# The scratch of queries, keys, values and gates stored in the order in which the attention stage reads it

## The chip, the cores and the metric

The kernel runs on one NeuronCore of a Trainium2 chip. The metric is device time of one execution in microseconds (us). Every engine has its own queue: TensorE (PE, with its weight loads as PEld), VectorE (DVE), ScalarE (ACT), GpSimd (POOL) and SyncE (SP). SP computes nothing here; it issues nearly all DMA transfers, in a fixed order, and a transfer whose data or buffer isn't ready holds up everything behind it on SP.

## What is computed

One decoder layer on x of 1024 positions by 1024 channels, in float32, and a final RMSNorm. What matters for this change is the attention branch; the rest is the work around it.

```
proj = h @ w_in[l]                       # h: x normed, scaled, shifted
q, k, v, g_attn, xr, g_rnn, m_attn, m_rnn = split(proj)
q = partial_rope(q, positions)           # 16 heads of 64, the first 16 columns turned
k = partial_rope(k, positions)           # 4 key heads; 4 query heads share each
y_attn = sliding_window_attention_with_sinks(q, k, v, sinks) * silu(g_attn)
y_rnn  = rg_lru(causal_conv(xr), ...) * silu(g_rnn)
merged = sigmoid(m_attn) * (y_attn @ w_attn_proj) + sigmoid(m_rnn) * (y_rnn @ w_rnn_proj)
out = rmsnorm(x + gate * (merged @ w_out), final_g)
```

The window is 128 positions: a block of 128 queries sees the keys of its own block and of the block before.

## The kernel before

**Numbers.** A float32 matrix is used as a high part, rounded to float32r, plus a low part, the rest; a product is made of three matmuls (high by high, low by high, high by low). That is why ACT (high parts, L100 and L102) and DVE (low parts, L106 and L108) work all the time beside PE.

**Stages.** The start (0 to about 97 us) norms and transposes x and makes the keys, v and the first gate products. Then a long run of products (`Pair`, `run`, L647) makes everything that comes from `w_in`, a pair of 128-column chunks at a time, with steps for ACT, DVE and SP hung on slots (`at_slot`). The queries of the four groups g come first in it (up to about 210 us), the attention gates from 433 to 586 us. From about 560 us the attention runs, 32 units u of one group and one block of 128 queries, and between its steps the last products and then the projection of the other branch (`rp_steps`, L169) fill PE. After 750 us come the attention projection, the merge and the output projection (L1707).

**The order of the work** is written out: each engine runs its instructions in the order in which the code issues them, and a group of instructions on different engines is tied by semaphores. SP's transfers take turns on eight semaphores (DMAHW0 to DMAHW7 in the rows below), so that a transfer isn't issued before the one eight places ahead of it has landed. POOL's transfers do the same (DMASW).

**Scratch in HBM.** Results that a later stage needs are stored to HBM and loaded again:

- `k_d` [512, 1024]: the keys of all heads, rows 0 to 255 high parts and 256 to 511 low parts. Written by `rope_a` and `rope_b` (L561, L577): each call makes 128 rows by 512 positions of a high part (`rhi`, ACT, L583) and of a low part (`rlo`, DVE, L587) and stores both.
- `q_d[g]` [512, 1024]: the same for the queries of group g.
- `vs_d[g]`, `dv_d[g]` [128, 8, 128]: v and the difference between v and v of the block before, made by `v_prep` (L1119), which reads v back from `v_d`.
- `ga_d[g]` [2, 128, 1024]: the gates, stored by `tanh_sinks` (L752) through `store`.

`rhi` and `rlo` have two buffers each, so the third `rhi` can be made only when the store of the first has landed. The same ACT queue then makes high parts of weights, for which DVE and PE wait.

**Loads of the attention** (L1165 to L1183). `load_kq(m)` serves two units. The keys of one head are 64 rows in `ks`; they are needed in all 128 partitions, once beside the high and once beside the low parts of the queries, so two transfers load the same data into partitions 0 to 63 and 64 to 127, in pieces of 256 or 384 positions (1.0 or 1.5 KB). `qs` is loaded in pieces of 256 positions (1 KB), four to a partition. `load_v(m)` loads `dv` and `vs` from POOL's queue, in pieces of 512 B to 1 KB. `load_gq(m)` (L1395) loads gates in pieces of 1 KB. `scores` (L1190) multiplies them: per unit eight matmuls, whose moving operand is 256 keys in one stretch of `ks`. The rows y of the other branch (`yh`, `yl`, `load_y`, L1307) and its weights (`load_r`) are loaded on SP in between.

Of the kernel before, what the change touches and what calls it, by code (L numbers as in the profile page):

```python
# [22 lines left out]
P = 128  # L23
# [5 lines left out]
NG = 4  # L29
# [22 lines left out]
def tile_hybrid_block(ctx, tc, x, pk, rows, posr, posi, invf, c_row, w_ss, w_gate, w_main, w_v,  # L52
# [506 lines left out]

    def rope_a(src, th, dst):  # L560
# [17 lines left out]
    def rope_b(src, th, dst, r0=P):  # L578
# [6 lines left out]
        def f2():  # L585
            t["l"] = rpp.tile([P, HALF], F32R, tag="rl", name="rlo", bufs=2)
            V.tensor_tensor(out=t["l"][:], in0=src(), in1=f32(t["h"][:]), op=ALU.subtract)  # L587
            dma(dst[r0:r0 + P, SL[th]], t["h"][:])
            dma(dst[r0 + 2 * P:r0 + 3 * P, SL[th]], t["l"][:])
# [134 lines left out]
    def rope_q(g):  # L724
        return {"C11": lambda s: rope_a(s, 0, q_d[g]), "C12": (blk, lambda s: rope_a(
                    s, 1, q_d[g])),
                "C21": lambda s: rope_b(s, 0, q_d[g]), "C22": (blk, lambda s: rope_b(
                    s, 1, q_d[g])), "late": 11}
# [24 lines left out]
    def tanh_sinks(dst, silu, own=False):  # L753
        def steps(j, th):
            def sink(s):
# [361 lines left out]
    def v_prep(g):  # L1117
# [19 lines left out]
        def f3():  # L1137
            for n_, d_, dst in (("v", "vs", vs_d), ("d", "dv", dv_d)):
# [26 lines left out]
    def load_kq(m):  # L1165
        g, t0 = m // 4, (m % 4) * 256
        ks = W["kq"].tile([P, 2, 384], F32R, tag="ks", name="ks")
        kv = k_d.rearrange("(b a r j) t -> j (a r) b t", b=2, a=2, r=32, j=4)[g]
        lo = P if t0 == 0 else 0
        for rep in range(2):  # L1170
            dma(ks[rep * 64:(rep + 1) * 64, :, lo:], kv[:, :, t0 - P + lo:t0 + 256])
        qs = W["kq"].tile([P, 4, 256], F32R, tag="qs", name="qs")
        dma(qs[:], q_d[g].rearrange("(a j) t -> a j t", j=4)[:, :, t0:t0 + 256])
        U["kq", m] = ks, qs

    def load_v(m):
        g, n0 = m // 4, (m % 4) * 2
        vs = at.tile([P, 2, P], F32R, tag="vs", name="vs", bufs=2)
        dv = at.tile([P, 2, P], F32R, tag="dv", name="dv", bufs=2)
# [662 lines left out]
```

## Time and profile before

| | |
|---|---|
| median of 3 runs | 936.0 us (935.87, 936.0, 938.92) |
| the profiled execution | 940.08 us, of which 938.4 us from the first to the last instruction |
| PE busy | 916.0 us (98%) |
| PEld, DVE, ACT, POOL busy | 756.6, 678.8, 541.2, 125.9 us |
| granted TensorE clock, mean | 0.993 |
| moved by DMA | 164.73 MB in 80691 packets, mean 176 GB/s |

Times in the trace count from the first instruction. In a table of windows a row gives a stretch of time: for each engine its busy time and in brackets the number of instructions, then the granted TensorE clock (PEclk, 1.00 is full), the mean busy share of the 16 DMA engines (it can read a little over 1) and the GB/s that they moved. In a list of waits a row names the engine and instruction that sat idle, what it waited for, the idle time in total, how often, and the longest. A timeline row gives start, duration, engine, line and operation, and in square brackets the idle time before it and what ended it. SPq is SP's issuing of transfers. A matmul's end is modelled; with nothing to wait for, the matmuls of 128x512 start 0.23 us apart.

### The profile page before, as it was taken

How to read it: one execution, taken by the hardware profiler on the slowest of the kernel's cores; microseconds unless marked ns; L12 is line 12 of the kernel's file. 1: busy time of each engine (PE TensorE's matmuls, PEld its weight loads, DVE VectorE, ACT ScalarE, POOL GpSimd, SP SyncE). 2: the span in 40 equal slices, each digit the busy share in tenths (PEclk: the TensorE clock that was granted, in tenths of full speed). 3: DMA queues.
4: the chain of work that ended last, by engine and by line, in shares of the span. 5: the costliest groups of instructions: out<-in, count | busy, mean ns of one | idle time of the engine just before them, and what ended most of it. 6: DMA issues, size and time to landing. Idle time of an engine off the chain costs nothing.

```text
span 938.4 us, 12480 instructions
## 1 busy us (share of the span) xinstructions
PE 916.0 (98%) x4285; PEld 756.6 (81%) x4285; DVE 678.8 (72%) x999; ACT 541.2 (58%) x1050; POOL 125.9 (13%) x227
## 2 busy tenths in 40 slices
PE   6999989999999999999999999999999999999997
PEld 5689878788888888888888888887888888888886
DVE  5998587786668955985697697898999737656522
ACT  6866544555556855866595875887887622212311
POOL 4720050000000000000000001444454300000000
PEclk9899999999999999999999999999999999999999
DMA  9815577472332443352435158998656186436321
GB/s 350 337 56 202 180 258 236 143 254 108 113 113 90 145 135 102 120 203 67 136 107 188 68 200 249 324 352 226 216 175 188 57 321 216 162 131 218 133 76 68
DMA packets 80691, 164.73 MB, mean 176 GB/s; under 512 B 12418, under 2 KB 28818, under 8 KB 80628
## 3 DMA queue, kind: packets, MB, share of 16 engines
q1 hardware_dynamic: 77876, 156.59, 49.4%
q0 software_dynamic: 2608, 7.09, 2.3%
q8 instruction: 34, 0.56, 0.2%
q14 instruction: 29, 0.24, 0.1%
q10 hardware_dynamic: 144, 0.26, 0.1%
HBM read 114.52 MB, written 49.78 MB: 175 GB/s over the span
## 4 chain that ended last, share of the span: by engine, by line
PE 79%; DMA 9%; DVE 6%; ACT 3%; issue 2%; SPq 0%; POOL 0%; DVEq 0%; ACTq 0%
PE bk L647 42%; PE rp L169 8%; PE pgate L956 5%; PE rp L1707 5%; PE pmain L1707 4%; PE s_ps L1200 3%; PE pmain L453 2%; PE pv L1273 2%; PE bk L453 2%; DMA tt<-tr_d 1%; DMA wo<-w_out 1%; DMA yl<-yl_d 1%; PE pt L1239 1%; DMA r<-w_rp 1%; DMA ks<-k_d 1%
## 5 line engine op out<-in xcount | busy, mean ns | idle before, releaser
L647 PE MATMUL bk<-nl,wh 128*128 128x512 f32 x368 | 144.5, 393 | 0.0
L647 PE MATMUL bk<-nh,wh 128*128 128x512 f32 x368 | 144.5, 393 | 0.0
L647 PE MATMUL bk<-nh,wl 128*128 128x512 f32 x368 | 143.6, 390 | 0.0
L106 DVE TENSOR_TENSOR wl<-r,wh 128x512 fp32r<-128x512 f32 x109 | 78.4, 726 | 13.1 <-ACT wh L100 13.1
L100 ACT CAST wh<-r 128x512 fp32r<-128x512 f32 x105 | 64.5, 618 | 34.7 <-DMA r<-w_ap 10.6
L647 PEld LDWEIGHTS bk<-nh,wl 128*128 128x128 f32 x368 | 69.1, 188 | 15.6
L647 PEld LDWEIGHTS bk<-nl,wh 128*128 128x128 f32 x368 | 69.1, 188 | 15.3
L647 PEld LDWEIGHTS bk<-nh,wh 128*128 128x128 f32 x368 | 69.2, 188 | 15.2 <-ACT wh L102 0.9
L647 PE MATMUL bk<-hl,wh 128*128 128x512 f32 x184 | 72.2, 393 | 0.0
L647 PE MATMUL bk<-hh,wh 128*128 128x512 f32 x184 | 72.2, 392 | 0.0
L647 PE MATMUL bk<-hh,wl 128*128 128x512 f32 x184 | 71.7, 390 | 0.0
L106 DVE TENSOR_TENSOR wl<-ws,wh 128x512 fp32r<-128x512 f32 x76 | 51.4, 682 | 4.8 <-ACT wh L100 4.8
L1225 ACT ACTIVATE p<-p,small 128x129 f32<-128x129 f32 x128 | 50.1, 401 | 0.0
L100 ACT CAST wh<-ws 128x512 fp32r<-128x512 f32 x76 | 45.7, 615 | 3.0 <-DVE ws L669 1.5
L821 POOL MEMSET xr<- 128x3 f32 x8 | 0.8, 100 | 313.2 <-PE pgate L956 232.8
L647 PEld LDWEIGHTS bk<-hl,wh 128*128 128x128 f32 x184 | 34.6, 188 | 7.7
L647 PEld LDWEIGHTS bk<-hh,wl 128*128 128x128 f32 x184 | 34.6, 188 | 7.7
L647 PEld LDWEIGHTS bk<-hh,wh 128*128 128x128 f32 x184 | 34.6, 188 | 7.2
L647 PE MATMUL bk<-hha,wl 128*128 128x512 f32 x92 | 36.9, 401 | 3.4 <-DVE wl L106 2.7
L1200 PE MATMUL s_ps<-ks,qs 128*128 128x256 f32 (+1 forms) x256 | 37.6, 289 | 0.3 <-DVE p L1215 0.3
L647 PE MATMUL bk<-hla,wh 128*128 128x512 f32 x92 | 36.8, 400 | 0.0
L760 ACT ACTIVATE c<-bk 128x512 f32<-128x512 f32 x29 | 17.3, 596 | 33.7 <-PE bk L647 33.7
(351 smaller groups left out, 2276.4 us busy)
## 6 DMA issues: line engine op xcount, KB each, us to landing
r<-w_main SPq DMA_DIRECT2D x100, 256.0 KB, 4.2
wada<-w_ss SPq DMA_DIRECT2D x16, 512.0 KB, 8.6
qs<-q_d SPq DMA_DIRECT2D x16, 512.0 KB, 5.6
ks<-k_d SPq DMA_DIRECT2D x24, 192.0 KB, 4.1
xt<-x SPq DMA_DIRECT2D x8, 512.0 KB, 8.2
sma_d<-c SPq DMA_DIRECT2D x16, 256.0 KB, 2.9
wg<-w_gate SPq DMA_DIRECT2D x8, 512.0 KB, 4.8
q_d<-rhi SPq DMA_DIRECT2D x16, 256.0 KB, 4.8
```

The costliest lines, as they stand in the source:

```text
L100: A.copy(dst[0][:], src)
L106: V.tensor_tensor(out=dst[1][:], in0=src, in1=f32(dst[0][:]), op=ALU.subtract)
L169: mm = T.matmul(ps[hf], ww, xx[kc][hf], start=(kc == 0 and ww is w_h and xx is xh), stop=(kc == KC - 1 and xx is xl))
L453: T.matmul(starts[c][hf], ww[:, c0:c0 + P], xh[kc][hf], start=(kc == 0 and t_ == "h"), stop=(kc == KC - 1 and t_ == "l"))
L647: W["pe"] = T.matmul(ps, ww[:, c], b[kc][xx_], start=(first and kc == 0 and i == 0), stop=(kc == 3 and i == 2), skip_group_check=not first)
L760: A.activation(t["t"], s(), AF.Tanh, scale=0.5)
L956: W["pe"] = T.matmul(ps[:, SL[hf]], ww[:, c0:c0 + P], xx_[:, SL[hf]], start=(ic == 0 and i == 0), stop=(ic == 1 and i == 2))
L1200: W["pe"] = T.matmul(o, qs[:, j, qc], ks[:, b, k0 + (0 if n else P):k0 + 256], start=(b == 0), stop=(b == 1))
L1225: A.activation(px[:, j, :], px[:, j, :], AF.Exp, bias=sm[:, 0, j:j + 1], accum_out=sm[:, 1, j:j + 1])
L1239: W["pe"] = T.transpose(pt[:, j, :], px[:, j, 0:P], ident[:])
L1273: W["pe"] = T.matmul(pv[:], b, m[:].rearrange("p j q -> p (j q)"), start=(i == 0), stop=(i == len(prods) - 1))
L1707: T.matmul(ps[:, sl], lhs[k][th][:, ts_], w[:, sl], start=(k == 0 and w is h_ and lhs is mh), stop=(k == KC - 1 and lhs is ml))
```

## The change

Four layouts in HBM change, and with them how they are written and read:

- `k_d` becomes [512, 8, 2, 128]: rows in which the same 64 keys stand twice, so that 128 rows belong to one head, and in a row, for each block of 128 positions, 128 high parts and then 128 low parts. Each store of keys becomes two of the same data, in pieces of 512 B. `ks` is one load of 128 rows, in pieces of 2 or 3 KB. In the scores the moving operand of 256 keys is now two stretches of 128, with the low (or high) parts of a block between them.
- `q_d[g]` becomes [4, 512, 256]: the positions in four parts of 256. A store writes pieces of 1 KB (2 KB before), `qs` is read in one piece of 4 KB a partition.
- `vs_d` and `dv_d` become one, `vd_d[g]` [128, 8, 2, 128], with a block's `dv` beside the block before's v. They are stored in pieces of 512 B (4 KB before) and loaded by one transfer in pieces of 2 KB, two transfers at a group's first block.
- `ga_d[g]` becomes [4, 128, 2, 256]: stored in pieces of 1 KB (2 KB before), loaded in pieces of 2 KB.

No instruction on PE, DVE or ACT is added, removed or moved. On SP eight stores of keys become sixteen and thirty-two loads of keys sixteen; on POOL thirty-two loads of v become twenty.

```diff
-    k_d = tc.dram_tile([512, S], F32, name="k_d")
+    k_d = tc.dram_tile([512, 8, 2, P], F32, name="k_d")
-    vs_d = [tc.dram_tile([P, 8, P], F32, name=f"vs_d{g}") for g in range(NG)]
-    dv_d = [tc.dram_tile([P, 8, P], F32, name=f"dv_d{g}") for g in range(NG)]
+    vd_d = [tc.dram_tile([P, 8, 2, P], F32, name=f"vd_d{g}") for g in range(NG)]
-    q_d = [tc.dram_tile([512, S], F32, name=f"q_d{g}") for g in range(NG)]
-    ga_d = [tc.dram_tile([2, P, S], F32, name=f"ga_d{g}") for g in range(NG)]
+    q_d = [tc.dram_tile([4, 512, 256], F32, name=f"q_d{g}") for g in range(NG)]
+    ga_d = [tc.dram_tile([4, P, 2, 256], F32, name=f"ga_d{g}") for g in range(NG)]
...
+    def to_k(r0, b, th):
+        return [(k_d[r:r + P, 4 * th:4 * th + 4, b, :], P) for r in (r0, r0 + 2 * P)]
+
+    def to_q(g):
+        def of(r0, b, th):
+            r = slice(r0 + 2 * P * b, r0 + 2 * P * b + P)
+            return [(q_d[g][2 * th:2 * th + 2, r, :].rearrange("m p t -> p m t"), 256)]
+        return of
...
-            dma(dst[r0:r0 + P, SL[th]], t["h"][:])
-            dma(dst[r0 + 2 * P:r0 + 3 * P, SL[th]], t["l"][:])
+            for b, n_ in enumerate("hl"):
+                for o, s_ in dst(r0, b, th):
+                    dma(o, t[n_][:].rearrange("p (n t) -> p n t", t=s_))
...
-                    store(dst[j][:, SL[th]], t["t"])
+                    if isinstance(dst, list):
+                        store(dst[j][:, SL[th]], t["t"])
+                    else:
+                        store(dst[2 * th:2 * th + 2, :, j, :].rearrange("m p t -> p m t"),
+                              t["t"].rearrange("p (m t) -> p m t", m=2))
...
-                dma(dst[g], t[d_][:])
+            dma(vd_d[g][:, 1:8, 1, :], t["vs"][:, 0:7, :])
+            dma(vd_d[g][:, :, 0, :], t["dv"][:])
...
-        ks = W["kq"].tile([P, 2, 384], F32R, tag="ks", name="ks")
-        kv = k_d.rearrange("(b a r j) t -> j (a r) b t", b=2, a=2, r=32, j=4)[g]
-        lo = P if t0 == 0 else 0
-        for rep in range(2):
-            dma(ks[rep * 64:(rep + 1) * 64, :, lo:], kv[:, :, t0 - P + lo:t0 + 256])
+        ks = W["kq"].tile([P, 3, 2, P], F32R, tag="ks", name="ks")
+        kv = k_d.rearrange("(p j) n b t -> j p n b t", j=4)[g]
+        n0 = t0 // P
+        lo = 1 if t0 == 0 else 0
+        dma(ks[:, lo:, :, :], kv[:, n0 - 1 + lo:n0 + 2, :, :])
         qs = W["kq"].tile([P, 4, 256], F32R, tag="qs", name="qs")
-        dma(qs[:], q_d[g].rearrange("(a j) t -> a j t", j=4)[:, :, t0:t0 + 256])
+        dma(qs[:], q_d[g][m % 4].rearrange("(a j) t -> a j t", j=4))
...
-        dma(dv[:], dv_d[g][:, n0:n0 + 2, :], G)
-        lo = 0 if n0 else 1
-        dma(vs[:, lo:, :], vs_d[g][:, n0 - 1 + lo:n0 + 1, :], G)
-        U["v", m] = vs, dv
+        vd = at.tile([P, 2, 2, P], F32R, tag="vd", name="vd", bufs=2)
+        if n0:
+            dma(vd[:], vd_d[g][:, n0:n0 + 2, :, :], G)
+        else:
+            dma(vd[:, 0, 0, :], vd_d[g][:, 0, 0, :], G)
+            dma(vd[:, 1, :, :], vd_d[g][:, 1, :, :], G)
...
-                W["pe"] = T.matmul(o, qs[:, j, qc], ks[:, b, k0 + (0 if n else P):k0 + 256],
+                W["pe"] = T.matmul(o, qs[:, j, qc], ks[:, kb:n % 2 + 2, b, :],
...
-        t = load_half(ga_d[g].rearrange("a p t -> p a t")[:, :, t0:t0 + 256])
+        t = load_half(ga_d[g][m % 4])
```

Two places on SP show what this does to its queue. The first is in the attention, where the first group ends: the loads of gates (`ga_d0` into r), keys, queries and of the rows y (hha2 and the like are buffers that hold y's high and low parts), before the change. In a row, what is loaded stands ahead of the arrow, then the shape, then the semaphores on which SP waits.

```order
L59 DMA r_5368<-ga_d0_94 128x2x256 [waits DMAHW0_49,Activation_49]
L59 DMA ks_5380<-k_d_79 64x2x384 [waits DMAHW1_49,PE_49]
L59 DMA ks_5380<-k_d_79 64x2x384 [waits DMAHW2_49]
L59 DMA qs_5383<-q_d0_90 128x4x256 [waits DMAHW3_49]
L59 DMA hha2_163<-yh_d1_115 128x512 [waits DMAHW4_49]
L59 DMA hla2_165<-yl_d1_123 128x512 [waits DMAHW5_49]
L59 DMA hha3_167<-yh_d1_115 128x512 [waits DMAHW6_49]
L59 DMA hla3_169<-yl_d1_123 128x512 [waits DMAHW7_49]
L59 DMA r_5508<-ga_d0_94 128x2x256 [waits DMAHW0_49,DVE_49,Activation_49]
L59 DMA ks_5520<-k_d_79 64x2x256 [waits DMAHW1_49,PE_49]
L59 DMA ks_5520<-k_d_79 64x2x256 [waits DMAHW2_49]
L59 DMA qs_5523<-q_d1_91 128x4x256 [waits DMAHW3_49]
```

The same stretch after the change:

```order
L59 DMA r_5368<-ga_d0_90 128x512 [waits DMAHW5_49,Activation_49]
L59 DMA ks_5380<-k_d_79 128x768 [waits DMAHW6_49,PE_49]
L59 DMA qs_5382<-q_d0_86 128x1024 [waits DMAHW7_49]
L59 DMA hha2_159<-yh_d1_111 128x512 [waits DMAHW0_49]
L59 DMA hla2_161<-yl_d1_119 128x512 [waits DMAHW1_49]
L59 DMA hha3_163<-yh_d1_111 128x512 [waits DMAHW2_49]
L59 DMA hla3_165<-yl_d1_119 128x512 [waits DMAHW3_49]
L59 DMA r_5505<-ga_d0_90 128x512 [waits DMAHW4_49,DVE_49,Activation_49]
L59 DMA ks_5517<-k_d_79 128x512 [waits DMAHW5_49,PE_49]
L59 DMA qs_5519<-q_d1_87 128x1024 [waits DMAHW6_49]
```

Each pair of key loads is one transfer now, so a load of queries or of y follows one semaphore turn earlier; the waits on PE, DVE and ACT are the same.

The second place is where the queries of group 0 (`q_d0`) and v of group 0 are stored on SP, between loads of weights (r, wg), before the change:

```order
L59 DMA q_d0_90<-rhi_1345 128x512 [waits DMAHW0_49,Activation_49]
L59 DMA q_d0_90<-rlo_1371 128x512 [waits DVE_49]
L59 DMA r_1383<-w_main 128x512 [waits DMAHW2_49]
L59 DMA q_d0_90<-rhi_1369 128x512 [waits DMAHW3_49,Activation_49]
L59 DMA q_d0_90<-rlo_1400 128x512 [waits DMAHW4_49,DVE_49]
L59 DMA r_1408<-w_main 128x512 [waits DMAHW5_49]
L59 DMA wg_1431<-w_gate 128x1024 [waits DMAHW6_49,DVE_49]
L59 DMA vs_d0_81<-vs_1270 128x1024 [waits DMAHW7_49,DVE_49]
L59 DMA dv_d0_85<-dv_1271 128x1024 [waits DMAHW0_49,DVE_49]
L59 DMA v32_1437<-v_d_80 128x8x64 [waits DMAHW1_49]
L59 DMA q_d0_90<-rhi_1423 128x512 [waits DMAHW2_49,Activation_49]
L59 DMA q_d0_90<-rlo_1451 128x512 [waits DMAHW3_49,DVE_49]
```

The same stretch after the change:

```order
L59 DMA q_d0_86<-rhi_1349 128x2x256 [waits DMAHW0_49,Activation_49]
L59 DMA q_d0_86<-rlo_1375 128x2x256 [waits DVE_49]
L59 DMA r_1387<-w_main 128x512 [waits DMAHW2_49]
L59 DMA q_d0_86<-rhi_1373 128x2x256 [waits DMAHW3_49,Activation_49]
L59 DMA q_d0_86<-rlo_1404 128x2x256 [waits DMAHW4_49,DVE_49]
L59 DMA r_1412<-w_main 128x512 [waits DMAHW5_49]
L59 DMA wg_1435<-w_gate 128x1024 [waits DMAHW6_49,DVE_49]
L59 DMA vd_d0_81<-vs_1274 128x7x128 [waits DMAHW7_49,DVE_49]
L59 DMA vd_d0_81<-dv_1275 1024x1x128 [waits DMAHW0_49,DVE_49]
L59 DMA v32_1441<-v_d_80 128x8x64 [waits DMAHW1_49]
L59 DMA q_d0_86<-rhi_1427 128x2x256 [waits DMAHW2_49,Activation_49]
L59 DMA q_d0_86<-rlo_1455 128x2x256 [waits DMAHW3_49,DVE_49]
```

The order and the waits are the same; only the shapes of the stores differ, 128x2x256 for a store of queries (256 pieces of 1 KB) and 7 or 8 pieces of 512 B to a row of v.

More of the change, by code (lines that the diff above doesn't have):

```diff
@@ L724, in rope_q @@
     def rope_q(g):
[L725 to L728, printed above, removed]
+        return {"C11": lambda s: rope_a(s, 0, to_q(g)), "C12": (blk, lambda s: rope_a(
+                    s, 1, to_q(g))),
+                "C21": lambda s: rope_b(s, 0, to_q(g)), "C22": (blk, lambda s: rope_b(
+                    s, 1, to_q(g))), "late": 11}
     behind, own_stores = [], []
@@ L1137, in f3 @@
         def f3():
-            for n_, d_, dst in (("v", "vs", vs_d), ("d", "dv", dv_d)):
+            for n_, d_ in (("v", "vs"), ("d", "dv")):
                 V.tensor_tensor(out=t[d_][:, :, 64:128], in0=t[n_][:],
                                 in1=f32(t[d_][:, :, 0:64]), op=ALU.subtract)
-                dma(dst[g], t[d_][:])
+            dma(vd_d[g][:, 1:8, 1, :], t["vs"][:, 0:7, :])
+            dma(vd_d[g][:, :, 0, :], t["dv"][:])
         waiting[1].extend([[("S", 0, 0, f0)], slots(4), [("D", 0, 0.85, f1)],
@@ L1177, in load_v @@
         g, n0 = m // 4, (m % 4) * 2
[L1178 to L1183 removed]
+        vd = at.tile([P, 2, 2, P], F32R, tag="vd", name="vd", bufs=2)
[4 more added lines that the diff above has]
+            dma(vd[:, 1, :, :], vd_d[g][:, 1, :, :], G)
+        U["v", m] = vd
     def sink(u):
@@ L1193, in scores @@
         qc = slice((n % 2) * P, (n % 2 + 1) * P)
-        k0 = (n % 2) * P
+        kb = n % 2 + (0 if n else 1)
         s_full = psx.tile([P, 1024], F32, tag="s", name="s_ps")
@@ L1266, in values @@
         n = u % 8
-        vs, dv = U["v", u // 2]
+        vd = U["v", u // 2]
         full, masked = U.pop(("m", u))
-        prods = [((vs if n else dv)[:, n % 2, :], m) for m in full]
-        prods += [(dv[:, n % 2, :], m) for m in masked]
+        prods = [(vd[:, n % 2, 1 if n else 0, :], m) for m in full]
+        prods += [(vd[:, n % 2, 0, :], m) for m in masked]
         pv = psx.tile([P, 4 * P], F32, tag="v", name="pv")
@@ L1484, in tile_hybrid_block @@
     wv.append(half(rv[1]))
-    now(rope_a(lambda: starts[0][0], 0, k_d))
+    now(rope_a(lambda: starts[0][0], 0, to_k))
     for c in range(2, 4):
@@ L1489, in tile_hybrid_block @@
     wv.append(half(rv[2]))
-    now(rope_a(lambda: starts[0][1], 1, k_d))
+    now(rope_a(lambda: starts[0][1], 1, to_k))
     wv.append(half(rv[3]))
@@ L1494, in tile_hybrid_block @@
     for hf in range(2):
-        now(rope_b(lambda: starts[1][hf], hf, k_d))
+        now(rope_b(lambda: starts[1][hf], hf, to_k))
     begin(-6)
```

## The prediction

> **What bounds the kernel now.** I read the table of windows over the whole program first, to see where PE ever stands still; then PE's waits; then, at the two places where DMA is behind a wait, the timelines of PE, ACT and SP; and last short windows, for how fast the DMA moves which transfers. The table, with the stages that matter here:
>
> ```profile
> 60.00:110.00 50.00, 50.00 (x313) 45.09 (x312) 35.68 (x50) 26.39 (x43) 0.55 (x3) 1.00 0.50 170
> 110.00:160.00 50.00, 46.71 (x196) 37.52 (x195) 41.64 (x64) 24.55 (x44) 12.30 (x25) 0.97 0.67 231
> 160.00:210.00 50.00, 50.00 (x216) 39.44 (x215) 40.19 (x67) 26.75 (x47) 0.10 (x1) 1.00 0.58 195
> ...
> 600.00:640.00 40.00, 38.43 (x209) 31.54 (x208) 36.42 (x66) 31.49 (x100) 17.47 (x32) 1.00 1.05 335
> 640.00:680.00 40.00, 40.00 (x221) 34.06 (x220) 35.90 (x65) 33.31 (x106) 18.15 (x31) 1.00 0.69 213
> ```
>
> PE is the bound. From 60 us to the end of the attention it is busy in every window but two: it loses 3.3 us between 110 and 160, and 1.6 us between 600 and 640, where the 16 DMA engines are busy without a gap (1.05). No edit touches PE's work, so the change can pay only through these two gaps, or cost by new ones. PE's waits over the whole trace, those of DMA and the longest behind the start:
>
> ```profile
> PE bk L647 <- DVE wl L106: 2.7, 1, 2.7
> PE rp L169 <- DMA yl<-yl_d: 1.1, 1, 1.1
> ...
> PE rp L169 <- DMA yh<-yh_d: 0.2, 1, 0.2
> ```
>
> In the attention the loads of scratch that the change reshapes (ks, qs, gates, v) never end a wait of PE themselves. What is late there is y, queued on the same engines. PE's timeline at that place:
>
> ```profile
> 634.25 0.63 PE L169 MATMUL rp<-yl,wh 128*128 128x512 f32 x2
> 635.12 0.73 PE L169 MATMUL rp<-yh,wh 128*128 128x512 f32 x2 [0.25 <-DMA yh<-yh_d]
> 635.69 0.63 PE L169 MATMUL rp<-yh,wl 128*128 128x512 f32 x2
> 637.39 0.73 PE L169 MATMUL rp<-yl,wh 128*128 128x512 f32 x2 [1.07 <-DMA yl<-yl_d]
> ```
>
> Two matmuls take 0.46 us from start to start. The pair at 635.12 comes 0.41 us late (635.12 - 634.25 - 0.46), the one at 637.39 1.24 us late. Sum 1.65 us; this is all that PE loses to DMA in the attention.
>
> **The loads: a gain of 1.65 us.** Whether y comes earlier depends on how fast the queue ahead of it drains. Short windows of the attention, one in which loads of keys and queries go through, then one in which rows of y do:
>
> ```profile
> 591.00:595.00 4.00, 4.00 (x24) 3.46 (x23) 3.42 (x7) 3.35 (x12) 2.02 (x4) 1.00 1.09 213
> ...
> 607.00:611.00 4.00, 4.00 (x22) 3.12 (x20) 3.30 (x6) 3.94 (x14) 2.82 (x5) 1.00 1.03 409
> ```
>
> The engines are full in both, but move 213 GB/s where pieces of 1 and 1.5 KB pass, which lie 4 KB or more apart, and 409 where rows of 4 KB pass. Which transfers stand ahead of y, SP's timeline says:
>
> ```profile
> 607.63 1.29 SPq L59 DMA_DIRECT2D ks<-k_d  x2
> 608.97 1.00 SPq L59 DMA_DIRECT2D qs<-q_d  x1
> ...
> 618.50 1.80 SPq L59 DMA_DIRECT2D ks<-k_d  x2
> 620.99 0.54 SPq L59 DMA_DIRECT2D qs<-q_d  x1
> ...
> 626.17 0.32 SPq L59 DMA_DIRECT2D yl<-yl_d  x1
> ```
>
> A load of keys and queries is 2 x 192 KB and 512 KB, 0.92 MB: 4.3 us at 213 GB/s, 2.2 us at 409. After the change qs is one stretch of 4 KB rows, so I take 409 for it; ks has 3 KB pieces 32 KB apart, unlike any row here, so between the two rates. By both at 409 the two loads ahead of yl save 4.2 us, by qs alone 2 x 1.2 = 2.4 us. Either is more than the 1.24 us that yl is late, and SP issues two transfers fewer ahead of it, which with turns on eight semaphores can only bring it forward. So the 1.65 us goes. What is late next: nothing of DMA, for from 640 on the share is 0.69 or less and PE's 40 us hold no gap.
>
> [...]
>
> The sixteen transfers that SP saves, and the twelve on POOL, I take at nothing: PE waits for POOL in no row of its list. That could be some tenths too low.
>
> **The stores: a cost of 0.1 us.** They happen where PE's larger gap is. What makes that gap, in ACT's timeline, then DVE's, then PE's:
>
> ```profile
> 128.54 0.59 ACT L583 CAST rhi<-bk 128x512 fp32r<-128x512 f32 x1 [5.29 <-DMA q_d<-rhi]
> ...
> 129.16 0.69 DVE L587 TENSOR_TENSOR rlo<-bk,rhi 128x512 fp32r<-128x512 f32 x1 [2.30 <-ACT rhi L583]
> ...
> 133.29 0.39 PE L647 MATMUL bk<-hha,wh 128*128 128x512 f32 x1
> 136.41 0.70 PE L647 MATMUL bk<-hha,wl 128*128 128x512 f32 x1 [2.73 <-DVE wl L106]
> ```
>
> ACT can't make the next `rhi` before a store of queries, two buffers back, has landed. It stands for 5.3 us, DVE behind it, then the weights' low part, and PE is 2.9 us late (136.41 - 133.29 - 0.23). SP's queue says what lies ahead of that store, which is the one at 121.36:
>
> ```profile
> 119.49 0.33 SPq L59 DMA_DIRECT2D q_d<-rlo  x1
> 119.87 0.92 SPq L59 DMA_DIRECT2D r<-w_main  x2
> ...
> 121.36 0.38 SPq L59 DMA_DIRECT2D q_d<-rhi  x1
> ...
> 127.12 0.33 SPq L59 DMA_DIRECT2D vs_d<-vs  x1
> ```
>
> So every tenth by which these two stores of queries (a load of w_gate lies between them too) slow, PE loses. No store in pieces of 1 KB is in the trace. Near rows are transfers of 256 KB, from the list of issues (median us from issue to landing):
>
> ```profile
> r<-w_main SPq DMA_DIRECT2D x100, 256.0 KB, 4.2
> v<-v_d SPq DMA_DIRECT2D x4, 256.0 KB, 4.6
> ```
>
> A row of w_main comes in 128 pieces of 2 KB, v in 1024 pieces of 256 B: 0.4 us for 896 pieces more, so 0.06 us for the 128 that a store of queries gains. Two stores: 0.1 us, which I take, since the pieces of v are smaller and still cost no more. From above: if 1 KB pieces went at 213 GB/s, 256 KB would take 1.2 us for 0.6, so 1.2 us for two. From below there is a reason for a gain too: the old stores write 2 KB of every 4 KB, the new ones two whole stretches of 128 KB, and the queue was slow while they passed:
>
> ```profile
> 121.00:124.00 3.00, 3.00 (x15) 2.46 (x14) 3.00 (x7) 2.12 (x4) 1.21 (x1) 1.00 0.81 162
> 125.00:130.00 5.00, 5.00 (x23) 4.13 (x22) 2.70 (x6) 1.46 (x3) 4.11 (x12) 1.00 1.04 401
> ```
>
> At 401 GB/s the 0.49 MB of that first stretch would take 1.2 us, so up to 1.8 us are there to be won, if the stores are the cause and not the two loads of weights beside them.
>
> The other stores: `vd_d` in 512 B pieces adds, by the same 0.06 us for 128, about 0.4 us to each of eight. The first pair is issued behind the gap's store (127.12 above), and ACT's later waits for a store of queries, between 140 and 215, leave no gap on PE:
>
> ```profile
> ACT rhi L583 <- DMA q_d<-rhi: 3.3, 2, 1.8
> ```
>
> So they are covered; if they weren't, each would cost up to those 0.4 us. The keys' stores, with loads of weights behind them on SP, and DVE's first use of those weights:
>
> ```profile
> 70.24 0.33 SPq L59 DMA_DIRECT2D k_d<-rhi  x1
> ...
> 81.20 1.45 SPq L59 DMA_DIRECT2D r<-w_main  x3
> ...
> 89.16 0.68 DVE L669 TENSOR_TENSOR ws<-r 128x512 f32<-128x512 f32 x1
> ```
>
> Eight issues more are 2.6 us of SP over those 11 us, of which the last store's two alone must push the loads, 0.7 us. The loads land 4.2 us after their issue by the median above, DVE takes them after 8: covered by some 3 us, beyond which each us would cost one. The gates are stored long before they are loaded.
>
> **The scores' moving operand** in two stretches: nothing, since the array takes the same 256 columns. The bound above is in the rivals; below nothing I see no reason.
>
> **The sum.** -1.65 + 0.1 = -1.55 us. On the profiled execution's own time: 940.08 - 1.55 = 938.5. That execution is 4.1 us above the median of the runs shown; I take the difference to stay, and forecast 936.0 - 1.55 = 934.4 us. A change of 0.5%, 4.7 us, is about what a measurement of this kernel can tell from none; the three runs lie 3 us apart. So the forecast is no change that shows.
>
> **The rivals.**
>
> (B) *Nothing comes of it.* yl is held by something else, such as its buffer or the y rows ahead of it, and the gap moves to the next load. For: SP's own waits between 585 and 640 are partly for PE. Against: the engines are full all the time, and the wait for PE's scores, row below, is spread over four loads. 936.0.
>
> ```profile
> SPq L59 <- PE s_ps L1200: 5.7, 4, 3.2
> ```
>
> (C) *The gap at 133 closes.* The stores land earlier by the 1.8 us. What hangs on it is more than the gap:
>
> ```profile
> 130.00:140.00 10.00, 7.27 (x25) 5.46 (x24) 9.11 (x15) 6.05 (x11) 5.98 (x13) 0.83 0.81 301
> 140.00:150.00 10.00, 10.00 (x45) 8.19 (x44) 9.97 (x16) 4.51 (x8) 0.00 (x0) 1.00 0.83 273
> ```
>
> The granted clock is 0.83 in the gap's ten us: 1.7 us of full clock are lost beside the idle time. [...] If a shorter gap leaves the clock alone, 1.8 + 1.7 = 3.5 us go, and with the loads 936.0 - 1.65 - 3.5 = 930.9. Against: the loads of weights (two of 256 KB, 2 KB of every 4 KB) are in the same queue and stay.
>
> (D) *The stores slow and PE pays: slower.* At the upper price, 1.2 us for the stores ahead of a wait, at all three places where ACT waits for a store of queries (5.3 us, and twice in the 3.3): 936.0 - 1.65 + 3.5 = 937.9. It decides from 0.6 us a place on. For: the later two waits are as near to PE as the first was. Against: the row of v.
>
> (E) *The moving operand costs: much slower.* If two stretches of 128 cost as two matmuls, a unit's eight would take as sixteen. From the chain of waits, eight with 256 columns and four with 128:
>
> ```profile
> 578.67 0.96 PE s_ps L1200 x8
> ...
> 586.19 0.44 PE pt L1239 x4
> ```
>
> 16 x 0.11 - 0.96 = 0.8 us in each of 28 units, 22 us: 956. No row shows such an operand; but the number of columns is the same.
>
> **How the numbers follow.** Forecast 0.68, B 0.12, C 0.08, D 0.08, E 0.04. Faster by over 0.5% (below 931.3): C, 0.08. Slower by over 0.5% (above 940.7): E, and D where the loads gain nothing and the stores of v add to it, 0.07. Within: 0.85. The range goes from 931.0, where the lower bound of the stores takes effect almost whole, to 938.2, just over D; it leaves out E, most of C and D's far end, some 0.15.
>
> **What would show it.** Right: in the attention no window of full engines below some 330 GB/s; no wait of PE for yl or yh between 600 and 640, and 40.0 us busy there; the wait near 133 as long as before within some tenths. Wrong: a first wait of PE for ks, qs or vd; a gap of PE between 140 and 215; scores that take longer than 0.96 us for eight; a wait for yl that is still there although the queue drains faster.

## The result, and the profile after

The changed kernel takes 934.92 us (median of 20 runs, 932.87 to 938.79), the kernel before 937.0 in the same session (20 runs, 934.48 to 940.27). The ratio is 0.9976, 95% interval 0.9965 to 0.9987: a gain of 2.2 us, 1.2 to 3.3. The prediction had 934.4 us, and -1.55 against before. The profiled execution took 935.74 us, with a span of 933.8 (before 940.08 and 938.4).

The windows of the changed kernel that answer to those shown of before (the columns are the same):

```profile
60.00:110.00 50.00, 49.74 (x312) 44.19 (x311) 37.25 (x53) 27.39 (x46) 0.59 (x2) 1.00 0.66 210
110.00:160.00 50.00, 47.41 (x199) 38.14 (x198) 42.70 (x66) 24.35 (x43) 12.46 (x25) 0.97 0.77 244
600.00:640.00 40.00, 39.90 (x220) 33.69 (x219) 37.90 (x69) 33.56 (x109) 19.04 (x30) 1.00 0.92 339
```

Between 600 and 640 PE is busy 39.9 us for 38.43, and the engines of the DMA are no longer full on average (0.92 for 1.05). PE's list of waits has no row left for yl or yh; its longest rows behind the start are:

```profile
PE bk L656 <- DVE wl L106: 1.8, 1, 1.8
PE rp L1722 <- ACT wo L1657: 1.1, 1, 1.1
PE bk L656 <- DVE wl L108: 0.8, 1, 0.8
```

PE's timeline, at the place where the pairs at 635.12 and 637.39 had been late, and then two rows of before that the comparison needs:

```profile
630.49 0.63 PE L168 MATMUL rp<-yl,wh 128*128 128x512 f32 x2
630.96 0.63 PE L168 MATMUL rp<-yh,wh 128*128 128x512 f32 x2
...
632.36 0.39 PE L1288 MATMUL pv<-phc,vd 128*128 128x512 f32 x1
...
633.65 1.19 PE L1215 MATMUL s_ps<-ks,qs 128*128 128x256 f32 x8
```

```profile
637.96 0.39 PE L1273 MATMUL pv<-phc,vs 128*128 128x512 f32 x1
...
639.24 1.19 PE L1200 MATMUL s_ps<-ks,qs 128*128 128x256 f32 x8
```

From the pair with yl to the first `pv` it was 3.71 us (637.96 - 634.25), now 1.87 (632.36 - 630.49): 1.84 us gone, for 1.65 forecast. The eight scores take 1.19 us in both. SP between 585 and 640 now waits for the buffers that PE frees, 22.3 us, and hardly for transfers (before, its rows for yl and yh had 6.5 and 3.7 us):

```profile
SPq L59 <- PE s_ps L1215: 22.3, 5, 7.1
...
SPq L59 <- DMA yl<-yl_d: 0.4, 1, 0.4
```

PE's idle time between 110 and 160 is two gaps in both kernels, and its list has a row for each. One, near 112, ends with the making of a low part at L108. The other, near 133, ends with one at L106 and is the gap that the prediction describes. The rows of the changed kernel, then that of before for the first gap (for the second it is the prediction's row at 136.41):

```profile
111.89 0.50 PE L656 MATMUL bk<-hha,wl 128*128 128x512 f32 x1 [0.84 <-DVE wl L108]
133.14 0.50 PE L656 MATMUL bk<-hha,wl 128*128 128x512 f32 x1 [1.75 <-DVE wl L106]
```

```profile
114.11 0.51 PE L647 MATMUL bk<-hha,wl 128*128 128x512 f32 x1 [0.56 <-DVE wl L108]
```

So the gap near 133 is 1.75 us for 2.73. The chain that makes it is the same. ACT's wait for the store of queries was 5.29 us and is now:

```profile
125.26 0.59 ACT L591 CAST rhi<-bk 128x512 fp32r<-128x512 f32 x1 [4.23 <-DMA q_d<-rhi]
```

**What of the difference is the change's.** The two spans lie 4.6 us apart, more than the runs' medians. The same matmul, just behind the start, in before and in the changed kernel, then one in the attention:

```profile
54.48 0.39 PE L453 MATMUL bk<-hh,wh 128*128 128x512 f32 x1
...
644.33 0.36 PE L1200 MATMUL s_ps<-ks,qs 128*128 128x256 f32 x1
```

```profile
51.61 0.39 PE L452 MATMUL bk<-hh,wh 128*128 128x512 f32 x1
...
638.74 0.36 PE L1215 MATMUL s_ps<-ks,qs 128*128 128x256 f32 x1
```

At 54 us, where nothing had been touched, it was ahead by 2.87 us already; at 644 by 5.59; at the end of the span by 4.6. Every kernel below was 1.8 to 3.2 us ahead there as well, so that start belongs to this one profile of before. Of the 2.7 us between the landmarks, 2.2 came behind 600 us, where the lead was still 3.4; the rest came near 133. Behind 644 about 1 us was lost again: in the output projection PE waits 1.1 us for `wo`, 0.2 before. The kernels below have 0 to 1.6 us there, in no order that goes with their layouts, so this isn't shown to be the change's.

### The profile page after: what moved, and what is told of

It reads as the page before. It is cut to its first block, busy times and chain, and to the rows that moved or that the text cites. A ratio compares the mean times of both kernels' runs of the same rounds, so it can differ in the third digit from the quotient of the medians.

```text
span 933.8 us, 12432 instructions
## 1 busy us (share of the span) xinstructions
PE 912.6 (98%) x4285; PEld 754.4 (81%) x4285; DVE 678.6 (73%) x999; ACT 540.8 (58%) x1050; POOL 121.2 (13%) x215
## 4 chain that ended last, share of the span: by engine, by line
PE 81%; DVE 8%; DMA 6%; ACT 2%; issue 2%; SPq 1%; POOL 0%; DVEq 0%; ACTq 0%
PE bk L656 44%; PE rp L168 13%; PE pgate L969 5%; PE rp L1722 5%; PE pmain L1722 4%; PE pmain L168 4%; PE s_ps L1215 3%; DMA r<-w_main 3%; PE pv L1288 3%; PE pt L1254 1%; DVE wl L106 1%; DMA xt<-x 1%; DVE jk L251 1%; DMA smr_d<-c 1%; DMA wg<-w_gate 1%
## 5 line engine op out<-in xcount | busy, mean ns | idle before, releaser
L106 DVE TENSOR_TENSOR wl<-r,wh 128x512 fp32r<-128x512 f32 x109 | 78.9, 731 | 15.5 <-ACT wh L100 15.5
L106 DVE TENSOR_TENSOR wl<-ws,wh 128x512 fp32r<-128x512 f32 x76 | 51.4, 683 | 4.4 <-ACT wh L100 4.4
```

The costliest lines, as they stand in the source:

```text
L106: V.tensor_tensor(out=dst[1][:], in0=src, in1=f32(dst[0][:]), op=ALU.subtract)
```

## The experiments

**Which part of the change empties the queue?** The prediction's theory R: the queue drained at 213 GB/s because of short pieces 4 KB apart. Rival T: the number of SP's transfers, on eight semaphores. The first four kernels: the queries' layout alone, the keys' alone, the old layout with rows 4.25 KB apart, and the change with two half loads of keys.

```diff
 q_only: before, with only
-    q_d = [tc.dram_tile([512, S], F32, name=f"q_d{g}") for g in range(NG)]
+    q_d = [tc.dram_tile([4, 512, 256], F32, name=f"q_d{g}") for g in range(NG)]
 ...                                         # and its stores and loads
 k_only: before, with only
-    k_d = tc.dram_tile([512, S], F32, name="k_d")
+    k_d = tc.dram_tile([512, 8, 2, P], F32, name="k_d")
 ...                                         # and its stores, loads and the scores' operand
 padded: before, with
-    k_d = tc.dram_tile([512, S], F32, name="k_d")
+    k_d = tc.dram_tile([512, S + 64], F32, name="k_d")
 ...                                         # and q_d the same
 after_halves: the changed kernel, with
-        dma(ks[:, lo:, :, :], kv[:, n0 - 1 + lo:n0 + 2, :, :])
+        for i in range(2):
+            h = slice(64 * i, 64 * i + 64)
+            dma(ks[h, lo:, :, :], kv[h, n0 - 1 + lo:n0 + 2, :, :])
```

> Only the queries' scratch and its loads are changed; keys, v and gates as before, so SP issues as many transfers as before. Theory R (rate): y is late in the attention because the loads of queries and keys move at half the rate of 4 KB rows. Then qs alone wins 2 x 1.2 = 2.4 us of queue ahead of yl, more than the 1.24 us that it is late: PE busy 39.7 us or more between 600 and 640, no wait of PE for yl or yh, ratio to before about 0.998. Theory T (turns): the gain is SP's, which issues 16 transfers fewer on eight semaphores. Then the gap stays, 38.4 to 39.0 us busy, ratio 1.000. Theory S (stores): the gain is the gap near 133, where the stores of queries land earlier. Then the gap of 600 to 640 says nothing, and PE's idle time between 110 and 160 falls below 2.6 us from 3.3.

> Only the keys' scratch and its loads are changed. Theory R: a load of keys (0.38 MB) takes 1.0 us at 409 GB/s for 1.8 us at 213, two ahead of yl win at most 1.7 us: the gap between 600 and 640 shrinks to 0 to 0.7 us (39.3 to 40.0 us busy). Theory T: it is gone whole, since all sixteen transfers that SP saves are here; with R refuted by the queries alone this is what T needs. Theory S: nothing changes near 133, 3.3 us idle between 110 and 160, and no gain. The moving operand in two stretches is in this kernel: eight matmuls of the scores take 0.96 us as before, or up to 1.76 us if a stretch costs as a matmul.

> Before, with the rows of the queries' and keys' scratch 256 B longer (4.25 KB apart, not 4 KB); every piece and every transfer has the length and the place in its queue that it had. If the low rate comes from the distance of the pieces, loads of keys and queries now pass at over 330 GB/s, the gap between 600 and 640 goes (39.7 us busy or more) and the time is that of the change, ratio about 0.998. If it comes from the length of the pieces, windows of 210 to 270 GB/s with full engines remain there, and the gap of 1.2 to 1.7 us with them, ratio 1.000.

> After, with the load of keys split into two transfers of 64 partitions again: the layouts are those of after, the number of SP's transfers in the attention that of before. Theory R: as after, 39.8 us or more busy between 600 and 640, ratio about 0.998. Theory T: the gap comes back, under 39.0 us busy, ratio 0.9995 to 1.000.

The window of 600 to 640 in these four, in the same order, one fence for each:

```profile
600.00:640.00 40.00, 39.42 (x216) 33.01 (x216) 37.24 (x68) 32.79 (x107) 20.11 (x33) 1.00 1.02 332
```

```profile
600.00:640.00 40.00, 39.90 (x219) 33.74 (x218) 37.42 (x68) 34.30 (x109) 20.63 (x33) 1.00 0.94 335
```

```profile
600.00:640.00 40.00, 37.82 (x196) 31.17 (x195) 35.12 (x64) 30.64 (x98) 18.58 (x30) 0.96 1.00 321
```

```profile
600.00:640.00 40.00, 38.33 (x203) 31.20 (x202) 36.24 (x66) 31.90 (x102) 16.22 (x28) 1.00 0.96 318
```

| | median, us | ratio to before, interval |
|---|---|---|
| q_only | 936.0 | 0.9992 (0.9976 to 1.0008) |
| k_only | 935.5 | 0.998 (0.9963 to 0.9996) |
| padded | 937.06 | 0.9997 (0.9982 to 1.0013) |
| after_halves | 936.55 | 0.9993 (0.9974 to 1.0012) |

The medians of each table come from sessions of their own, in which the kernel before had 937.67 us here and 937.95 to 939.04 further down, so kernels are compared by the ratio.

The keys' part alone does it: 39.90 us busy. The queries' part leaves 0.6 us. That the rows lie 4 KB apart isn't the cause: with 4.25 KB the gap is as wide as before, or wider. And the change with two half loads has the gap back, though its queries are one stretch and its keys come in pieces of 3 KB. R fell there; but T was left standing, and a new theory stood beside it, H: a load that writes only partitions 0 to 63, or 64 to 127, passes at about half rate (239 and 232 GB/s in two windows of after_halves that are shown below). So three more kernels: the change with each load of keys in two parts by position, over all partitions (before's number of transfers, no half); the same in two parts of 64 partitions, the even and the odd, which lose as much as the halves if it is the number of partitions that counts, and nothing if it is which; and the kernel before with one edit, keys stored twice in the old rows.

```diff
 after_blocks: the changed kernel, with
-        dma(ks[:, lo:, :, :], kv[:, n0 - 1 + lo:n0 + 2, :, :])
+        for i in (slice(lo, 2), slice(2, 3)):
+            dma(ks[:, i, :, :], kv[:, n0 - 1 + i.start:n0 - 1 + i.stop, :, :])
 after_evenodd: the changed kernel, with
-        dma(ks[:, lo:, :, :], kv[:, n0 - 1 + lo:n0 + 2, :, :])
+        for i in range(2):
+            dma(ks[i::2, lo:, :, :], kv[i::2, n0 - 1 + lo:n0 + 2, :, :])
 k_twice: before, with
-    k_d = tc.dram_tile([512, S], F32, name="k_d")
+    k_d = tc.dram_tile([512, 2, S], F32, name="k_d")
 ...                                         # each store goes to two places
-        for rep in range(2):
-            dma(ks[rep * 64:(rep + 1) * 64, :, lo:], kv[:, :, t0 - P + lo:t0 + 256])
+        dma(ks[:, :, lo:], kv[:, :, t0 - P + lo:t0 + 256])
```

> The changed kernel with each load of keys split in two by position, each over all 128 partitions (256 or 128 positions first, 128 then). It issues as many transfers of keys as the kernel before, but none goes to half of the partitions. Theory H (a load that writes 64 partitions only passes at about half rate): nothing is lost, PE busy 39.9 to 40.0 us of 600 to 640, no wait for yl or yh above 0.1, no window of full engines below 330 GB/s, median 934.9. Theory T (what delayed y was the number of transfers on SP's turns): the gap is back as with the halves, PE busy about 38.3, waits for yl and yh of 1 to 1.5 us together, median about 936.5. Theory R (short pieces): pieces of 2 and 1 KB instead of 3, so a part of the gap, 0.3 to 0.8 us.

> The changed kernel with each load of keys split in two, one into the partitions of even number and one into those of odd number, 64 each. Same bytes, same pieces of 3 KB, same number of transfers as the run with halves 0-63 and 64-127, which lost 1.6 us between 600 and 640 and showed windows of 213 to 264 GB/s. [...] Theory H2 (any load of 64 partitions is slow, because it has half the pieces to spread): as with the halves, PE busy 38.3, waits of 1 to 1.5 us, windows near 213 to 264. Theory T (number of transfers): as H2 in the gap, but windows at 360 or more. The last two differ in the windows.

> The kernel before with one edit: keys are stored twice, in the old rows of 4 KB, so that one load in pieces of 1 to 1.5 KB, the old ones, fills all 128 partitions; queries, v, gates, the keys' tile and the scores' moving operand (one stretch) as before. Theory H (half-partition loads): the whole gain of the attention, PE busy 39.9 to 40.0 of 600 to 640, no wait for yl or yh, windows with keys in flight at 330 GB/s or more, 2.0 to 2.3 us over the attention, median about 935 to 935.5. Theory R (short pieces far apart, the one of the prediction): pieces are as before, so PE busy about 38.4, waits of 1 to 1.3 us, median as before, 937. Theory T: 12 transfers fewer as in the change, so as H in the gap, but with windows of 213 to 270 GB/s still there.

| | median, us | ratio to before, interval | PE busy of 600 to 640 |
|---|---|---|---|
| after_blocks | 935.91 | 0.997 (0.9949 to 0.9991) | 39.90 |
| after_evenodd | 936.69 | 0.9976 (0.9957 to 0.9996) | 39.90 |
| k_twice | 935.87 | 0.9972 (0.9951 to 0.9993) | 39.88 |

None of the three has a row for yl or yh in PE's waits. T falls with the first: the transfers are as many as before, and nothing is lost. R falls again with the last: the pieces are the old 1 to 1.5 KB. And the second tells what a half is. In the two kernels with 64 partitions to a load only the loads of keys have pieces of 3 KB, so the packets in the trace tell in which windows keys pass. First two such windows of the halves 0-63 and 64-127 (after_halves), then two of even and odd (after_evenodd), with 94 to 128 pieces of keys in each:

```profile
619.00:623.00 4.00, 3.75 (x22) 3.11 (x21) 3.82 (x7) 3.41 (x12) 1.28 (x3) 1.00 1.07 239
...
631.00:635.00 4.00, 2.58 (x11) 1.48 (x10) 3.85 (x7) 2.98 (x11) 1.59 (x2) 1.00 1.03 232
```

```profile
619.00:623.00 4.00, 3.90 (x23) 3.18 (x22) 3.82 (x8) 2.75 (x9) 2.37 (x5) 1.00 1.05 406
...
627.00:631.00 4.00, 4.00 (x24) 3.42 (x23) 3.83 (x8) 3.21 (x13) 0.49 (x1) 1.00 1.07 368
```

The engines read as full in both, but move 239 and 232 GB/s against 406 and 368. Between these two windows, where no or few keys pass, the halves too move 368 and 383. (Even and odd have one window of full engines below 360 GB/s, 312 at 599, but no keys pass in it.) It isn't that they are 64 partitions, but which. Why the halves are slow, no run here shows.

**What makes the gap near 133?** The prediction held that every tenth by which the stores of queries slow, PE loses. Theory Q: it is the stores' place in SP's queue, behind loads of weights. Theory E: the 16 engines are full there, whatever the queue. Three kernels issue stores of queries from other queues: high parts on ACT's, then also the low parts on POOL's, then both on ACT's. Where their expectations add PE's waits of 1.8 and 0.8 us as near 133, only the first is; the second is the gap near 112.

```diff
 hi_act: the changed kernel, with
 ...
             A.copy(t["h"][:], src())
+            for o, s_ in dst(r0, 0, th):
+                dma(o, t["h"][:].rearrange("p (n t) -> p n t", t=s_),
+                    nc.sync if dst is to_k else nc.scalar)
 ...                                         # and only the low part's store stays as it was
 hi_act_lo_pool: that, and behind the low part's making
+                dma(o, t["l"][:].rearrange("p (n t) -> p n t", t=s_),
+                    nc.sync if dst is to_k else G)
 hilo_act: the changed kernel, with
-                    dma(o, t[n_][:].rearrange("p (n t) -> p n t", t=s_))
+                    dma(o, t[n_][:].rearrange("p (n t) -> p n t", t=s_),
+                        nc.sync if dst is to_k else nc.scalar)
```

> The changed kernel with the stores of the high parts of the queries issued on ACT's queue, straight behind the cast that makes them, instead of on SP's behind loads of weights. Theory Q (ACT's wait near 125, 4.2 us, is the place of the store in SP's queue): the store is issued some 1 us earlier and doesn't stand behind the loads, ACT's wait falls to under 1.5 us, the waits of PE for wl near 133 (1.8 and 0.8) go, the clock stays at 1.0 there, PE busy 49 to 50 of 110 to 160, and 2 to 3.5 us go: median 931.5 to 933. Theory E (the 16 engines are full there, whatever the queue): the wait stays within 1 us, PE busy 47 to 48, median 934.9. Against both: an issue takes 0.4 us of ACT, which has 24 of 50 us busy there; if it queues before the casts that PE waits for, 0.4 us each at worst.

> As the run with the high parts' stores on ACT's queue, where ACT's wait of 4.2 us for a store of queries went, but DVE then stood 2.6 us for the store of the low part, two buffers back, and PE 1.9 and 0.8 us as before. Here the low parts' stores go to POOL's queue, so that none of the queries' stores stands behind weights on SP. Theory Q2 (the place of both stores in SP's queue makes the gap): DVE's wait falls under 0.8 us, PE's waits for wl near 133 fall under 0.5 in sum, clock 1.0, PE busy 49 to 50 of 110 to 160, 2 to 3.5 us less than the change: 931.5 to 933. Theory E (the 16 engines are full from 120 to 135, at 1.0 to 1.1, so that what comes earlier delays something else): a wait for weights, ACT or DVE for r from w_main, takes the place, PE's waits stay at 1.5 us or more, median 934 to 935.

> As the last, but both parts' stores are issued by ACT, behind the making of the low part on DVE, so that ACT waits for DVE ahead of each pair of stores. Theory Q2: the gap of PE near 133 goes as there, unless ACT's waits for DVE, up to 1 us at each of 16 pairs, cost elsewhere between 100 and 215; median 931.5 to 934. Theory E: the gap stays, median 934 to 935, or later by what ACT waits.

| | median, us | ratio to before, interval | PE busy of 110 to 160 |
|---|---|---|---|
| hi_act | 933.9 | 0.9952 (0.9934 to 0.997) | 47.31 |
| hi_act_lo_pool | 939.63 | 1.0014 (0.9997 to 1.0031) | 45.20 |
| hilo_act | 936.26 | 0.9969 (0.9945 to 0.9993) | 46.17 |

In the first, ACT's wait for the store is gone, and PE's gap is as it was, for now DVE stands for the low part's. DVE's timeline, then PE's:

```profile
127.27 0.69 DVE L598 TENSOR_TENSOR rlo<-bk,rhi 128x512 fp32r<-128x512 f32 x1 [2.61 <-DMA q_d<-rlo]
```

```profile
133.53 0.50 PE L658 MATMUL bk<-hha,wl 128*128 128x512 f32 x1 [1.89 <-DVE wl L106]
```

With the low parts on POOL's queue the gap near 133 does close to 0.6 us, but a longer one opens behind it. PE's timeline, then DVE's and POOL's:

```profile
132.60 0.50 PE L659 MATMUL bk<-hha,wl 128*128 128x512 f32 x1 [0.61 <-DVE wl L106]
146.82 0.50 PE L659 MATMUL bk<-hh,wl 128*128 128x512 f32 x1 [2.96 <-DVE wl L106]
```

```profile
145.47 0.69 DVE L598 TENSOR_TENSOR rlo<-c,rhi 128x512 fp32r<-128x512 f32 x1 [5.55 <-DMA q_d<-rlo]
```

```profile
142.74 1.52 POOL L59 DMA_DIRECT2D q_d<-rlo  x2 [0.26 <-issue]
```

DVE made the first of these two low parts at 136.1, but POOL, busy with work of its own, issued the stores at 142.7. With both parts on ACT's queue DVE waits 2.9 us, ACT 5.1 and 3.6 us for DVE, and PE has 1.7 us near 134 and 1.6 more at 124.

So Q holds for the gap itself, when both stores leave SP's queue, and E, "whatever the queue", does not; but none of the three is shown to gain over the change by it. What hi_act's median has over the change is within the intervals, and its profile can't place it: it is of the slowest of its twelve runs (936.58 us).

That leaves the bytes: the changed kernel without six of the eight loads of w_gate (512 KB each), two of which stand at 118 and 123; and the changed kernel, with all its work, with the gate row begun five slots later.

```diff
 no_gate_loads: the changed kernel, with
         def load(c):
+            if 2 <= c < KC:
+                t[c] = t[c - 2]
+                return
 gate_late8: the changed kernel, with
-        waiting[0].append(slots(3))
+        waiting[0].append(slots(8))
```

> The changed kernel without six of the eight loads of w_gate (512 KB each; the rows loaded first are used again, so that the gate row is not the reference's). Two of these loads stand in SP's queue between 118 and 124, ahead of or beside the stores of queries that ACT waits for. All engines' work is as in the change. Theory E (the 16 DMA engines are full from 120 to 135; the gap of PE near 133 is a matter of bytes, not of the layout of the stores or of their queue): ACT's wait of 4.2 us near 125 falls under 2, PE's waits for wl of 1.8 and 0.8 us go under 0.5 in sum, clock 1.0 from 130 to 140, and with it 2.5 to 4 us: median 931 to 932.5. Theory S (the stores of queries are slow by themselves, whatever is beside them): the wait stays at 3.5 us or more, the gap at 1.5 or more, median 934 to 935.

> The changed kernel with the steps of the gate row begun five slots of 2.75 us later, so that no load of w_gate stands among the first two tiles of queries' stores; all work is kept, and DVE, ACT and SP take the gate row and the preparation of v in another order there. Theory E: the first gap closes as in the run without these loads, and unless the later stages, with DMA shares of 0.7 to 1.0, gain a gap of their own, the median is 931 to 933. A new wait of 0.5 to 2 us where the loads now stand, between 140 and 170, would leave 933 to 935. Theory S: no gain.

Without the loads the median is 933.88 us, ratio 0.9961 (0.9939 to 0.9983). ACT's wait is 1.88 us for 4.23, PE's gap near 133 is 0.57 us for 1.75, the gap near 112 stays, and the clock keeps 1.00. So theory S falls, and E comes out at this gap, if not quite to the 0.5 us that it forecast:

```profile
123.55 0.59 ACT L591 CAST rhi<-bk 128x512 fp32r<-128x512 f32 x1 [1.88 <-DMA q_d<-rhi]
```

```profile
112.52 0.51 PE L656 MATMUL bk<-hha,wl 128*128 128x512 f32 x1 [0.96 <-DVE wl L108]
132.62 0.50 PE L656 MATMUL bk<-hha,wl 128*128 128x512 f32 x1 [0.57 <-DVE wl L106]
```

```profile
130.00:140.00 10.00, 9.43 (x41) 7.42 (x41) 9.93 (x18) 5.24 (x11) 8.90 (x14) 1.00 0.52 151
```

The changed kernel in the same ten us:

```profile
130.00:140.00 10.00, 8.25 (x30) 6.28 (x29) 9.93 (x17) 5.32 (x10) 4.38 (x8) 0.83 0.91 250
```

41 matmuls for 30 in ten us: the idle time and the clock together. Begun later, the gate row closes the gap near 133 as well, but gains nothing: 937.82 us, ratio 0.9994 (0.9977 to 1.0011). The loads, and the order of ACT and DVE that moved with them, make two other gaps:

```profile
113.35 0.76 PE L656 MATMUL bk<-hha,wl 128*128 128x512 f32 x1 [1.90 <-DVE wl L108]
135.03 0.50 PE L656 MATMUL bk<-hha,wl 128*128 128x512 f32 x1 [0.57 <-DVE wl L106]
175.57 0.50 PE L656 MATMUL bk<-hha,wl 128*128 128x512 f32 x1 [1.82 <-DVE wl L108]
```

So three kernels, each by one profile, bring the gap near 133 to 0.6 us: both stores off SP's queue, the loads beside them gone, or the loads later. The stores land late there because they stand among these loads. How much of that is the place in the queue and how much the bytes isn't parted, for a load that is left out leaves the queue too.

No kernel here is shown to be faster than the change. k_twice, with its one edit, is as fast within what can be told.

## Why the prediction was right, point by point

**The bound and the two gaps: right.** PE is the bound, and only the gap of the attention closed. The 3.3 us between 110 and 160 are themselves two gaps (0.56 and 2.73), of which the working explains the second.

**The loads, -1.65 us: right in size, wrong in the reason.** The gap measured 1.84 us where it went, and of the windows of 4 us from 587 to 639 none with a DMA share of 1 or more reads below 378 GB/s, as was forecast. The failing step is the reading of the window with 213 GB/s: the prediction put it to "pieces of 1 and 1.5 KB", which lie 4 KB or more apart. padded has those pieces at another distance, and the gap; k_twice has them without the half loads, and no gap. The trace of before already spoke against it: in the window at 409 GB/s 226 pieces of 1 KB pass as well, at 46 ns each, and in that at 213 such a piece takes 90 ns. From this followed the step "by qs alone 2 x 1.2 = 2.4 us. Either is more than the 1.24 us": false. q_only left a wait of 0.5 us for yl, after_halves, with the same queries' layout, 1.0, and 0.4 for yh. Why these two differ by 0.9 us isn't shown; in the four kernels with half loads PE loses between 0.6 and 2.2 us of 600 to 640, so what q_only's profile has less than before's can't be put down to its layout. In the ten kernels with loads over all 128 partitions, the even and odd ones included, PE loses 0.1 us. The forecast came out because both readings fit the same windows, and the change removed the short pieces, the distance and the half loads together. As to the reason, that is luck.

**The 409 GB/s with which the loads' gain was worked out: reached.** In the changed kernel the queue moved 394 to 421 GB/s for 16 us on end:

```profile
607.00:611.00 4.00, 4.00 (x24) 3.25 (x24) 3.82 (x9) 3.76 (x12) 1.98 (x5) 1.00 1.03 421
611.00:615.00 4.00, 4.00 (x25) 3.44 (x24) 3.96 (x7) 3.47 (x12) 2.50 (x4) 1.00 1.03 408
615.00:619.00 4.00, 3.90 (x20) 3.05 (x19) 3.85 (x7) 2.81 (x12) 2.56 (x5) 1.00 1.04 394
619.00:623.00 4.00, 4.00 (x22) 3.41 (x22) 3.92 (x8) 3.35 (x11) 2.09 (x2) 1.00 1.02 396
```

**SP's fewer transfers at nothing: right**, by after_blocks.

**The stores of queries, +0.1 us: not to be told from nothing.** The gap near 133 is 1.75 us in the changed kernel for 2.73, a whole us shorter, where the prediction expected it as long as before within some tenths. But that isn't shown to be the layout's: with the new layout and the stores on SP the other kernels of the first question have 1.5 (after_blocks) to 2.25 (after_evenodd), with the old one 1.85 (padded) to 2.15 (k_only). The step behind it, that PE loses every tenth by which ACT's store slows, was too simple: hi_act took ACT's wait away, and DVE's took its place.

**The stores of v and keys: covered, the second with less to spare than said.** The lists of issues, before and after (KB each, median us to landing):

```profile
dv_d<-dv SPq DMA_DIRECT2D x4, 512.0 KB, 5.9
...
k_d<-rhi SPq DMA_DIRECT2D x4, 256.0 KB, 2.0
```

```profile
k_d<-rhi SPq DMA_DIRECT2D x8, 256.0 KB, 3.5
...
vd_d<-dv SPq DMA_DIRECT2D x4, 512.0 KB, 5.7
```

`vd_d` in 512 B pieces lands no later than `dv_d` did. The keys' stores land 1.5 us later (in k_twice, as many stores in pieces of 2 KB, 0.7), and push the weights behind them by more than the 0.7 us of the working. SP's issue of the first and last of them and of those weights, then DVE's first use:

```profile
68.99 0.93 SPq L59 DMA_DIRECT2D k_d<-rhi  x2
...
81.36 1.73 SPq L59 DMA_DIRECT2D k_d<-rlo  x2
83.13 2.33 SPq L59 DMA_DIRECT2D r<-w_main  x3
```

```profile
90.00 0.69 DVE L678 TENSOR_TENSOR ws<-r 128x512 f32<-128x512 f32 x1 [1.09 <-DMA r<-w_main]
```

From the first store of keys to these weights SP takes 14.1 us (83.13 - 68.99) for 11.0 before, so the stores cost it some 3.2 us. The cover of 3 us was used up, and DVE waits 1.1 us. PE doesn't: its only wait from 60 to 110 is 0.2 us, for something else.

**The moving operand, nothing: right.** 1.19 us for eight in both.

**The rivals.** B fell with the gap, D with PE's list of waits, E with the scores' 1.19 us. C was right that a lowered clock hangs on the gap; but the change didn't close the gap, and its window still has 0.83. From the matmul at 102 us to that at 153 the changed kernel is 0.75 us shorter than before. The five other kernels with 0.83 between 130 and 140 lie from 0.35 us longer to 0.7 shorter, and the five whose clock stays at 1.00 from 110 to 160 are 0.8 (hilo_act), 1.6 (padded) and 2.5 to 3.4 us shorter (q_only, after_blocks, no_gate_loads).

**"No change that shows": too careful.** Twenty runs of each do show it, with an interval of 1.2 to 3.3 us.

## What to carry to other kernels

Where the DMA engines read as full at a low rate (213 GB/s here), ask first which partitions the transfers write, and only then how long the pieces are: with pieces of keys of 3 KB in both, windows with loads of halves moved 232 and 239 GB/s, those with even and odd partitions 368 and 406. Here storing the keys twice, to load them once over all 128 partitions, gave as much as all four new layouts together, as far as times tell. The queries' layout alone was not shown to gain; those of v and the gates were not run alone. A reason that fits a window isn't tested by a change that removes several things at once; kernels with one of them each told it apart. Take the gaps of an engine one by one, by a timeline: two rows of a list of waits that look like one gap were 20 us apart here. And where all work was kept, each edit that closed the gap near 133 opened one of 1.8 to 3.0 us elsewhere.

## What the runs showed of the hardware

In windows of 4 us with full engines in which loads of 64 partitions pass beside other transfers, the engines moved 368 and 406 GB/s with the even and the odd partitions, 232 and 239 with the halves. The loads have the same bytes and pieces in both, and the busy share of 1.03 to 1.07 looks the same. Other transfers that were queued beside a half load were late with it: PE waited for y (0.5 to 2.0 us in the four kernels with half loads), not for keys.

In these fourteen profiles, from 60 us to the end of PE's work, the clock went nearly by the length of a single gap of PE. It kept 1.00 behind every gap of up to 1.72 us (hilo_act) that stood alone, and fell to 0.50 for 3.4 us behind all eight from 1.89 (hi_act) to 2.96 us (hi_act_lo_pool). In between the order breaks: 1.75 us (the changed kernel) lowered it, while 1.82 (gate_late8 at 176), 1.85 (padded) and 1.88 (q_only) did not. Two gaps in padded, 0.75 and 1.33 us long and 1.2 us apart, lowered it together, near 634. Within before and the changed kernel its changes lie whole multiples of 3.41 us apart (27.31, 136.54 and 139.95 us in before), so where a gap falls in these steps may count; what decides in the end no run here shows.
